# A 4096-cubed matmul with GELU on one core: more of its Strassen products split a second time

## The chip, the core and the metric

The kernel runs on one core of one Trainium2 chip. The metric is device time in microseconds, median of several executions. Single executions of one kernel agree within some 0.3%. A ratio is the mean time of one kernel's fast runs over that of the other's in the same rounds, so it is not quite the ratio of the medians quoted.

## The reference

```python
def reference(a, b):                      # float32, 4096 x 4096 each
    x = np.matmul(a, b)
    return 0.5 * x * (1 + np.tanh(np.sqrt(2 / np.pi) * (x + 0.044715 * x**3)))
```

## The kernel before

A and B are cut in quadrants and multiplied by Strassen's seven products (M1 to M7) in float16. The output is made in 16 groups, each a 512-row by 512-column tile of all four output quadrants. One product of one group is 64 matmuls of 128x128x512. It accumulates in one of two chains of four PSUM banks (the accumulators of TensorE), X or Y. A group goes in steps: a quarter of an unsplit product, or one of the half-sized products explained next.

From group 6 on, the right-hand operands come back from DRAM, where earlier groups kept them ("k_M", units of 1 MB), into a ring of eight 1 MB tiles ("bK"). A product can itself be split by Strassen into seven half-sized ones, 7/8 of the work. This is done for the pair M3/M5 in groups 11, 13, 14 and 15. For that, the first group that meets a set of columns after group 5 (the "maker": groups 6, 7, 9, 10) computes 14 right-hand halves of 0.5 MB. Ten of them are VectorE sums, made in one of three buffers "bS"; four are raw quarters. It writes all to DRAM ("k_split").

```python
SPLIT_GROUPS = (11, 13, 14, 15)
...
    def make_split(gi, s, p):
        blocks = [split_tiles[gi, nb, product(gi, s)[0], c] for c in range(CH)]
        o = SPLIT[p][2]
        if isinstance(o, str):
            t = quarter_b(blocks, o)
        else:
            t = pool.tile([P, 4 * NC], F16, name="bS", tag="bS", bufs=AHEAD + 1)   # 3 buffers
            take(t..., o[2], quarter_b(blocks, o[0]), quarter_b(blocks, o[1]))      # VectorE
        keep_operand((nb, "split", k // 2), k % 2, t)                               # SyncE queue
...
        makes = [                                     # one half of each product per step
            (position[gi, s + 1 + k // QPH, k % QPH], s, p)
            for s in (0, 1) for k, p in enumerate("1346725")
        ] if made else []
```

VectorE also makes the left-hand sums ("aS") that TensorE takes as weights, the joins of split products and the sums of the outputs, all in one order. The loads are issued by GpSimd, all writes by SyncE. Groups 9 and 10 also load A once more (float32, "stage"), to check the range of the inputs.

## Time and profile before

1574.95 us median of 3 runs (1574.2 to 1581.67). The profile shown has a span of 1580.3 us.

| | before |
|---|---|
| TensorE | 1561.8 us busy, 99% |
| VectorE | 1034.0 us, 65% |
| ScalarE | 656.7 us, 42% |
| DMA | 399.96 MB, 253 GB/s on average |

TensorE's busy time says that matmuls are running, not at what clock. The prediction shows the lines of each view. One more line shows groups 6 to 10 together; its columns are the stretch, its length, the busy time of TensorE, of weight loads, VectorE, ScalarE and GpSimd (with instructions), then the granted clock, the DMA share (the mean busy time of the 16 DMA engines over the stretch; it can come out above 1) and GB/s landed:

```profile
610.00:1102.00 492.00, 486.75 (x2242) 219.91 (x2241) 266.97 (x276) 208.54 (x650) 78.12 (x131) 0.99 0.99 284
```

### The profile page before, as it was taken

The numbers are of one execution on the slowest core, as the hardware profiler recorded it, in microseconds if no ns is written. First come the engines' busy times: TensorE is split into PE (matmuls) and PEld (weight loads), VectorE is DVE, ScalarE is ACT, GpSimd is POOL, SyncE is SP. The second block draws the span as 40 slices with busy tenths as digits, with TensorE's granted clock in tenths as the row PEclk, the third lists the DMA queues.
The fourth block names the chain that finished last, engine by engine and source line by source line (L and its number), as shares of the span: only waits on it lengthen the run. The fifth ranks groups of instructions, "written<-read, shape, count | busy, mean of one in ns | idle before, by whom it ended". The sixth has DMA issues, their size and how long they took to land. (4 is left out here: it accounts for less than half of the span.)

```text
span 1580.3 us, 21111 instructions
## 1 busy us (share of the span) xinstructions
PE 1561.8 (99%) x7630; PEld 748.3 (47%) x7630; DVE 1034.0 (65%) x1189; ACT 656.7 (42%) x1638; POOL 367.4 (23%) x652
## 2 busy tenths in 40 slices
PE   9999999999999999999999999999999999999998
PEld 4444444444444444444444444444644456474643
DVE  1697887969888886646454554476664574673853
ACT  1036444338874641212466435554456632121111
POOL 7763432331124300020222102201222101010100
PEclk9999999999999999999999999999999999999999
DMA  9999999994799986889999789999999667383752
GB/s 176 195 222 287 268 306 270 288 200 78 204 230 295 295 310 240 293 321 237 318 275 263 250 243 338 311 318 287 326 311 253 211 225 305 142 339 133 264 215 82
DMA packets 226336, 399.96 MB, mean 253 GB/s; under 512 B 17328, under 2 KB 156592, under 8 KB 204720
## 3 DMA queue, kind: packets, MB, share of 16 engines
q0 software_dynamic: 152704, 243.31, 65.1%
q1 hardware_dynamic: 73520, 155.22, 26.8%
q8 instruction: 62, 1.02, 0.2%
q14 instruction: 50, 0.41, 0.1%
HBM read 327.16 MB, written 155.19 MB: 305 GB/s over the span
## 5 line engine op out<-in xcount | busy, mean ns | idle before, releaser
L401 PEld LDWEIGHTS <-aS 128*128 128x128 f16 x4704 | 461.3, 98 | 565.9 <-issue 12.9
L401 PE MATMUL accX<-bK,aS 128*128 128x512 f16 x1664 | 360.9, 379 | 0.0
L763 DVE TENSOR_TENSOR aS<-aT 128x2048 f16<-128x2048 f16 x204 | 241.1, 1217 | 86.5 <-PE accX L401 57.8
L401 PE MATMUL accY<-bK,aS 128*128 128x512 f16 x1280 | 281.0, 382 | 5.2 <-DVE y L549 2.9
L401 PEld LDWEIGHTS <-aT 128*128 128x128 f16 x1728 | 169.3, 98 | 207.9 <-issue 4.8
L540 ACT ACTIVATE y<-y 128x512 f32<-128x512 f32 x192 | 119.0, 630 | 285.2 <-DVE y L549 285.1
L228 ACT ACTIVATE scrap<-stage 128x256 bf16<-128x256 f16 x512 | 212.8, 416 | 50.1 <-DMA stage<-in_a_dram 35.3
L206 POOL DMA_DIRECT2D bR<-in_b_dram x320 | 173.1, 544 | 208.0 <-DMA bR<-in_b_dram 112.5
L760 POOL DMA_DIRECT2D bK<-k_M x124 | 67.8, 548 | 515.7 <-PE accX L401 105.2
L206 POOL DMA_DIRECT2D stage<-in_a_dram x176 | 111.6, 642 | 231.0 <-ACT scrap L228 171.0
L365 DVE TENSOR_TENSOR aS<-aT 128x2048 f16<-128x2048 f16 (+1 forms) x112 | 133.9, 1200 | 34.6 <-PE accX L401 25.6
L401 PE MATMUL accX<-bS,aS 128*128 128x512 f16 x704 | 153.4, 379 | 1.3 <-ACT x L513 0.7
L513 ACT COPY x<-accX 128x512 f32<-128x512 f32 x128 | 74.6, 586 | 180.5 <-PE accX L401 174.4
L365 DVE TENSOR_TENSOR bS<-bR 128x2048 f16<-128x2048 f16 x110 | 133.6, 1217 | 16.6 <-PE accX L401 12.0
L250 ACT ACTIVATE square<-bR 128x1024 bf16<-128x1024 f16 x120 | 122.9, 1049 | 48.3 <-DVE energy L549 46.9
L401 PE MATMUL accX<-bK,aT 128*128 128x512 f16 x640 | 139.8, 379 | 0.0
L181 DVE STREAM_TRANSPOSE aT<-stage 128x2048 uint32<-128x2048 uint32 (+1 forms) x37 | 74.6, 2017 | 66.7 <-DMA stage<-in_a_dram 65.2
L513 ACT COPY m<-accX 128x512 f32<-128x512 f32 x60 | 34.5, 581 | 199.6 <-PE accX L401 179.3
L549 DVE TENSOR_TENSOR x<-x,x 128x512 f32<-128x512 f32 x64 | 43.7, 683 | 85.7 <-ACT x L513 85.7
L228 ACT ACTIVATION_READ_ACCUMULATOR scrap<-stage 128x1 f32 x512 | 95.5, 187 | 0.0
L549 DVE TENSOR_TENSOR energy<-energy,square 128x1024 bf16<-128x1024 bf16 x120 | 82.0, 683 | 9.7 <-ACT square L250 8.1
L549 DVE TENSOR_TENSOR x<-accX,x 128x512 f32<-128x512 f32 x64 | 43.6, 690 | 62.4 <-ACT y L540 56.0
(63 smaller groups left out, 1167.6 us busy)
## 6 DMA issues: line engine op xcount, KB each, us to landing
bK<-k_M POOLq DMA_DIRECT2D x124, 1024.0 KB, 10.5
out_dram<-y SPq DMA_DIRECT2D x256, 256.0 KB, 6.8
bR<-in_b_dram POOLq DMA_DIRECT2D x320, 128.0 KB, 7.5
k_M<-bS SPq DMA_DIRECT2D x80, 512.0 KB, 6.6
stage<-in_a_dram POOLq DMA_DIRECT2D x144, 256.0 KB, 10.6
bK<-k_split POOLq DMA_DIRECT2D x28, 1024.0 KB, 6.7
k_split<-bS SPq DMA_DIRECT2D x40, 512.0 KB, 4.8
k_M<-bR SPq DMA_DIRECT2D x16, 1024.0 KB, 12.1
```

The source lines that it names most:

```text
L181: nc.vector.transpose(dst[:, :, x, :], src[:, :, x, :])
L206: nc.gpsimd.dma_start(out=dst, in_=src)
L228: nc.scalar.activation(weighed[mb, quad, c][:, :RUN], s[:, x, :], ACT.Square, accum_out=weighed[mb, ih][:, k, x : x + 1])
L250: nc.scalar.activation(t[:, :], src, ACT.Square)
L365: nc.vector.tensor_tensor(out=x, in0=y, in1=z, op=ALU.add if o[2] > 0 else ALU.subtract)
L401: nc.tensor.matmul(acc[:, :], sa[:, j // 2, i * P : (i + 1) * P, j % 2], sb[:, j, :], start=start and j == 0, stop=stop and j == 3, skip_g ...
L513: nc.scalar.copy(out=t[:, :], in_=src[:, :])
L540: nc.scalar.activation(y[:, :], src[:, :], ACT.Gelu_apprx_tanh)
L549: nc.vector.tensor_tensor(out=o[:, :], in0=x[:, :], in1=y[:, :], op=op)
L760: nc.gpsimd.dma_start(out=t, in_=kept_unit(*key[1:])[:, :])
L763: nc.vector.tensor_tensor(out=t, in0=y, in1=z, op=ALU.add if op > 0 else ALU.subtract)
```

## The change

The intent is to give TensorE fewer matmul columns. M3/M5 are split in groups 8 and 12 too, and a second pair, M2/M1, in groups 6, 9, 10, 13 and 14. For these five groups the products stand in another order, in which M2 and M1 begin both PSUM chains anew. Each maker now makes 28 halves. A group that is both maker and user of M2/M1 makes them in its steps 1 to 5, reads them back a few steps later, and makes those of M3/M5 at its end, for which it loads M3 and M5 again.

```diff
+FRESH = [PRODUCTS[k] for k in (0, 1, 2)] + [
+    ("M2", "Y", ("21", "22", -1), "11"), PRODUCTS[3], ("M4", "Y", "22", ("21", "11", 1)),
+    ("M6", "X", ("21", "11", -1), ("11", "12", 1)),
+]
+MAKES = (1, 1, 1, 2, 2, 2, 3, 3, 3, 3, 4, 4, 5, 5)
-SPLIT_GROUPS = (11, 13, 14, 15)
+SPLITS = {M3_M5: (8, 11, 12, 13, 14, 15), M2_M1: (6, 9, 10, 13, 14)}
+LOAD_AHEAD = 10
...
-        if p in "24":
-            joins[chain, p] = pool.tile([P, NC], F32, name="join", tag="x1", bufs=RT)
+        if p == "2":
+            joins[chain] = pool.tile([P, NC], F32, name="join", tag="m5", bufs=2)
...
-        makes = [ (position[gi, s + 1 + k // QPH, k % QPH], s, p) for s in (0, 1) ... ]
+            if gi in SPLITS[M2_M1]:
+                orders = [(M2_M1, 3, 4, MAKES), (M3_M5, 0, 1, [step_number(gi, 5, 0) + x // 2 for x in range(14)])]
+            else:
+                orders = [
+                    (M3_M5, 0, 1, [step_number(gi, 2, 0) + x // 2 for x in range(14)]),
+                    (M2_M1, 5, 3, [step_number(gi, 6, 0) + x // 3 - 1 for x in range(14)]),
+                ]
... (settling of the new order, the planning of the ring, bank parity: left out)
```

More of the change, by code (lines that the diff above doesn't have):

```diff
@@ L56 @@
 PAIR = [(s, p) for ps in ("213", "45", "76") for s in (0, 1) for p in ps]
+MAKES = (1, 1, 1, 2, 2, 2, 3, 3, 3, 3, 4, 4, 5, 5)
+M3_M5, M2_M1 = 0, 3
 SPLIT_AHEAD = 6
 FETCH_AHEAD = 12
-SPLIT_GROUPS = (11, 13, 14, 15)
+SPLITS = {M3_M5: (8, 11, 12, 13, 14, 15), M2_M1: (6, 9, 10, 13, 14)}
+LOAD_AHEAD = 10
 CHECK_GROUP = 9
@@ L321, in product @@
     def product(gi, s):
-        return (LAST if gi == len(groups) - 1 else PRODUCTS)[s]
+        if gi == len(groups) - 1:
+            return LAST[s]
+        return (FRESH if gi in SPLITS[M2_M1] else PRODUCTS)[s]
     kept = {}
@@ L388, in half_path @@
     post = {}
+    x_banks = [0]
+    for gi in range(len(groups) - 1):
+        x_banks.append(x_banks[gi] if gi in SPLITS[M2_M1] else 1 - x_banks[gi])
     def bank(gi, chain, i):
-        par = (gi + (chain == "Y")) % 2
+        par = (x_banks[gi] + (chain == "Y")) % 2
         t = psum_pool.tile([P, NC], F32, name=f"acc{chain}", tag=f"bank{par}{i}")
@@ L454, in multiply @@
         name, chain = product(gi, s)[:2]
-        first = q == 0 and name in ("M3", "M5")
+        first = q == 0 and name in (("M3", "M5", "M2", "M1") if gi in SPLITS[M2_M1] else ("M3", "M5"))
         sa, sb = sums.pop((gi, s, q))
@@ L490, in multiply_split @@
                 settle(gi, name, i)
-        if p in "24":
-            joins[chain, p] = pool.tile([P, NC], F32, name="join", tag="x1", bufs=RT)
+        if p == "2":
+            joins[chain] = pool.tile([P, NC], F32, name="join", tag="m5", bufs=2)
         for r in range(RT // 2):
-            def join(p):
-                return joins[chain, p][:, r * NC // 2 : (r + 1) * NC // 2]
+            join = joins[chain][:, r * NC // 2 : (r + 1) * NC // 2]
             def joined(out, x, y, op):
@@ L500, in multiply_split @@
             if p == "2":
-                nc.scalar.copy(out=join("2"), in_=region(chain, "21", r))
+                nc.scalar.copy(out=join, in_=region(chain, "21", r))
             elif p == "3":
-                joined(join("2"), region(chain, "12", r), join("2"), ALU.subtract)
-                joined(join("2"), region(chain, "11", r), join("2"), ALU.add)
+                joined(join, region(chain, "12", r), join, ALU.subtract)
+                joined(join, region(chain, "11", r), join, ALU.add)
             elif p == "4":
-                nc.scalar.copy(out=region(chain, "22", r), in_=join("2"))
-                joined(join("4"), region(chain, "21", r), join("2"), ALU.add)
+                nc.scalar.copy(out=region(chain, "22", r), in_=join)
+                joined(join, region(chain, "21", r), join, ALU.add)
             elif p == "5":
-                joined(region(chain, "11", r), join("4"), region(chain, "12", r), ALU.subtract)
+                joined(region(chain, "11", r), join, region(chain, "12", r), ALU.subtract)
     def keep(tag, src, bufs):
@@ L554, in settle @@
         end = gi == len(groups) - 1
-        if name == "M5":
+        if gi in SPLITS[M2_M1] and name not in ("M5", "M7"):
+            settle_fresh(gi, name, i, X, Y)
+        elif name == "M5":
             if end:
@@ L587, in settle, with settle_fresh @@
             waiting.append((gi, i, 1, 1, y, y))
+    def settle_fresh(gi, name, i, X, Y):
+        if name == "M3":
+            post["x1", i] = keep("x1", Y, RT)
+        elif name == "M2":
+            m2, x1, x7 = keep("m5", Y, 2), post["x1", i], post["x7", i]
+            tt(x1, x1, m2, ALU.subtract)
+            tt(x7, x7, m2, ALU.subtract)
+        elif name == "M1":
+            m1, x7 = keep("m5", X, 2), post["x7", i]
+            tt(x7, x7, m1, ALU.add)
+        elif name == "M4":
+            emit(gi, i, 1, 0, new_y(), Y)
+            y = new_y()
+            tt(y, Y, post.pop(("x7", i)), ALU.add)
+            flush()
+            waiting.append((gi, i, 0, 0, y, y))
+        elif name == "M6":
+            y = new_y()
+            tt(y, X, post.pop(("x1", i)), ALU.add)
+            flush()
+            waiting.append((gi, i, 1, 1, y, y))
     steps = [(0, -1, n) for n in range(N_PLAIN)]
@@ L592, in half_path @@
     for gi in range(1, len(groups)):
-        if gi in SPLIT_GROUPS:
-            steps += [(gi, s, p) for s, p in PAIR]
-        else:
-            steps += [(gi, s, q) for s in (0, 1) for q in range(QPH)]
-        steps += [(gi, s, q) for s in range(2, NP) for q in range(QPH)]
+        s = 0
+        while s < NP:
+            if gi in SPLITS.get(s, ()):
+                steps += [(gi, s + x, p) for x, p in PAIR]
+                s += 2
+            else:
+                steps += [(gi, s, q) for q in range(QPH)]
+                s += 1
     position = {step: n for n, step in enumerate(steps)}
@@ L603, in step_number @@
         gi, s = gi + s // NP, s % NP
-        return position.get((gi, s, q), first_step[gi] + s * len(SPLIT) + 2 * q)
+        if (gi, s, q) in position:
+            return position[gi, s, q]
+        s0 = max(x for x in SPLITS if x <= s)
+        return position[gi, s0, PAIR[0][1]] + (s - s0) * len(SPLIT) + 2 * q
     def at(gi, s, q, fn, *args):
@@ L674, in do @@
             before.setdefault(n, []).append((fn, args))
+        free_at = [0, 0]
         for (quad, c), n in zip(chunks, turns):
-            do(n - 6, load, (load_a, (mb, quad, c)))
+            do(max(n - LOAD_AHEAD, free_at.pop(0)), load, (load_a, (mb, quad, c)))
+            free_at.append(n + 4)
             if turned:
@@ L736, in half_path @@
     )}
-    n_ring = 0
     tasks = {}
@@ L742, in task, with ring_place @@
         tasks.setdefault(n, []).append((fn, args))
-    def ring_place(need, ahead):
-        nonlocal n_ring
-        x = n_ring % len(ring)
-        n_ring += 1
-        n = max(ring_end[x] + 1, need - ahead)
+    owner = {}
+    def ring_place(need, ahead, key, after=0):
+        x = min(ring_end, key=ring_end.get)
+        n = max(ring_end[x] + 1, need - ahead, after)
         assert n <= need, (steps[need], steps[n])
+        owner[x] = key
+        ring_end[x] = need
         return x, n
@@ L771, in quarter_b, with blocks_a @@
         return tiles[k].rearrange("p (x y) -> p x y", x=NJ)[:, :, w * NC // 2 : (w + 1) * NC // 2]
-    def blocks_a(gi, o):
+    def blocks_a(gi, s, o):
         if isinstance(o, str):
@@ L777, in blocks_a, with open_block, block_sum @@
         return [
-            split_tiles["d", gi, c].rearrange("p (jj m) -> p jj m", jj=NJ // 2) for c in range(CH)
+            split_tiles["d", gi, s, c].rearrange("p (jj m) -> p jj m", jj=NJ // 2) for c in range(CH)
         ]
-    def open_block(gi, c, x):
-        split_tiles["d", gi, c] = ring_tile(x, "aD")
-    def block_sum(gi, o, q):
+    def open_block(gi, s, c, x):
+        split_tiles["d", gi, s, c] = ring_tile(x, "aD")
+    def block_sum(gi, s, o, q):
         w = 4 * NC
-        t = split_tiles["d", gi, q // 2][:, (q % 2) * w : (q % 2 + 1) * w]
+        t = split_tiles["d", gi, s, q // 2][:, (q % 2) * w : (q % 2 + 1) * w]
         mb = groups[gi][0]
@@ L795, in operand_a @@
             y, z, op = SPLIT[q][1]
-            blocks = blocks_a(gi, o)
+            blocks = blocks_a(gi, s, o)
             t = t.rearrange("p (jj m) -> p jj m", jj=NJ // 2)
@@ L811, in operands @@
             if sa is None:
-                sa = quarter_a(blocks_a(gi, oa), SPLIT[q][1])
-            k = PAIR.index((s, q))
-            sb = split_tiles[gi, nb, "split", k // 2][:, (k % 2) * w : (k % 2 + 1) * w]
+                sa = quarter_a(blocks_a(gi, s, oa), SPLIT[q][1])
+            k = PAIR.index((s - max(x for x in SPLITS if x <= s), q)) % 2
+            sb = split_tiles[split_key(gi, s, q)][:, k * w : (k + 1) * w]
         else:
@@ L823, in make_split @@
         nb = groups[gi][1]
-        blocks = [split_tiles[gi, nb, product(gi, s)[0], c] for c in range(CH)]
+        name = product(gi, s)[0]
+        blocks = [split_tiles[gi, nb, name, c] for c in range(CH)]
         o = SPLIT[p][2]
@@ L834, in make_split @@
             t = t[:, :]
-        k = PAIR.index((s, p))
-        keep_operand((nb, "split", k // 2), k % 2, t)
+        s0, x = {"M3": (M3_M5, 0), "M5": (M3_M5, 1), "M2": (M2_M1, 0), "M1": (M2_M1, 1)}[name]
+        k = PAIR.index((x, p))
+        keep_operand((nb, "split", s0, k // 2), k % 2, t)
     b_slot0 = dict(b_slot)
@@ L843, in half_path, with split_key, plan_fetch @@
     last_a = 0
+    made_at = {}
+    def split_key(gi, s, p):
+        s0 = max(x for x in SPLITS if x <= s)
+        return gi, groups[gi][1], "split", s0, PAIR.index((s - s0, p)) // 2
+    def plan_fetch(units, key, n, ahead):
+        if key not in units or owner[units[key]] != key:
+            units[key], e = ring_place(n, ahead, key, made_at.get(key[1:], -1) + 1)
+            task(e, fetch, key, units[key])
+        ring_end[units[key]] = max(ring_end[units[key]], n)
     for gi in range(N_RAW, len(groups)):
-        n0, nb = first_step[gi], groups[gi][1]
-        split = (gi, 0, "1") in position
+        nb = groups[gi][1]
         made = gi == maker[nb]
-        mine = [n for n in range(n0, first_step.get(gi + 1, len(steps)))]
+        mine = [n for n in range(first_step[gi], first_step.get(gi + 1, len(steps)))]
         ready = position[gi - 1, NP - 1, 2] if groups[gi][0] != groups[gi - 1][0] else 0
-        units, block_users = {}, []
-        makes = [
-            (position[gi, s + 1 + k // QPH, k % QPH], s, p)
-            for s in (0, 1) for k, p in enumerate("1346725")
-        ] if made else []
+        units, places, users = {}, {}, {}
+        makes = {}
+        if made:
+            if gi in SPLITS[M2_M1]:
+                orders = [(M2_M1, 3, 4, MAKES), (M3_M5, 0, 1, [step_number(gi, 5, 0) + x // 2 for x in range(14)])]
+            else:
+                orders = [
+                    (M3_M5, 0, 1, [step_number(gi, 2, 0) + x // 2 for x in range(14)]),
+                    (M2_M1, 5, 3, [step_number(gi, 6, 0) + x // 3 - 1 for x in range(14)]),
+                ]
+            for s0, y, x, whens in orders:
+                for k, ((z, p), n) in enumerate(zip(PAIR, whens)):
+                    if whens is MAKES:
+                        n += first_step[gi]
+                    makes.setdefault(n, []).append(((y, x)[z], p))
+                    made_at[nb, "split", s0, k // 2] = n
         for n in mine:
@@ L857, in half_path @@
             name, _, oa, ob = product(gi, s)
+            for sm, p in makes.get(n, ()):
+                for c in range(CH):
+                    key = (gi, nb, product(gi, sm)[0], c)
+                    plan_fetch(units, key, n, FETCH_AHEAD)
+                task(n, make_split, gi, sm, p)
+                if not isinstance(SPLIT[p][2], str):
+                    assert free["bS"][-AHEAD - 1] < n, steps[n]
+                    free["bS"].append(n)
             block = q in SPLIT and not isinstance(oa, str)
             if block and q == PAIR[0][1]:
-                places = [ring_place(n, SPLIT_AHEAD) for c in range(CH)]
-                e = max(ready, last_a, *(e for _, e in places))
-                for c, (x, _) in enumerate(places):
-                    task(e, open_block, gi, c, x)
+                places[s] = [ring_place(n, SPLIT_AHEAD, (gi, s, c)) for c in range(CH)]
+                users[s] = []
+                e = max(ready, last_a, *(e for _, e in places[s]))
+                for c, (x, _) in enumerate(places[s]):
+                    task(e, open_block, gi, s, c, x)
                 for qq in range(QPH):
-                    task(e, block_sum, gi, oa, qq)
+                    task(e, block_sum, gi, s, oa, qq)
                 last_a = e
@@ L870, in half_path @@
             if not isinstance(o, str):
-                tag = "aS" if made or n_a % 2 else "bS"
+                ahead = SPLIT_AHEAD if q in SPLIT else AHEAD
+                only = any(n - ahead <= x <= n for x in makes) or made and q not in SPLIT
+                tag = "aS" if only or n_a % 2 else "bS"
                 n_a += 1
-                e = max(n - (SPLIT_AHEAD if q in SPLIT else AHEAD), ready, last_a, free[tag][-AHEAD - 1] + 1)
+                e = max(n - ahead, ready, last_a, free[tag][-AHEAD - 1] + 1)
                 assert e <= n, steps[n]
@@ L878, in half_path @@
             if block:
-                block_users.append(max(e, n if isinstance(o, str) else 0))
-                for x, _ in places:
-                    ring_end[x] = max(block_users)
+                users[s].append(max(e, n if isinstance(o, str) else 0))
+                for x, _ in places[s]:
+                    ring_end[x] = max(users[s])
             task(n, operands, gi, s, q)
-            key = (gi, nb, "split", PAIR.index((s, q)) // 2) if q in SPLIT else (gi, nb, name, q // 2)
-            if key not in units:
-                units[key], e = ring_place(n, FETCH_AHEAD)
-                task(e, fetch, key, units[key])
-            ring_end[units[key]] = max(n, *(e for e, s1, _ in makes if s1 == s)) if s < 2 and made else n
-        for e, s, p in makes:
-            task(e, make_split, gi, s, p)
-            if not isinstance(SPLIT[p][2], str):
-                free["bS"].append(e)
+            key = split_key(gi, s, q) if q in SPLIT else (gi, nb, name, q // 2)
+            plan_fetch(units, key, n, FETCH_AHEAD)
     with tc.manual_schedule():
```

## The prediction

> **What bounds the kernel now.** I read the page's first two parts first: which engine is busy, and how evenly.
>
> ```profile
> PE 1561.8 (99%) x7630; PEld 748.3 (47%) x7630; DVE 1034.0 (65%) x1189; ACT 656.7 (42%) x1638; POOL 367.4 (23%) x652
> DMA  9999999994799986889999789999999667383752
> ```
>
> TensorE is busy 99% of the span with almost no holes, so today the number of matmul columns sets the time. But the second line says that the DMA engines are nearly as full in slices 11 to 31. The list of what TensorE waited for confirms the first: all its waits come to some 13 us, and the chain of waits is useless here (one Gelu).
>
> ```profile
> PE accY L401 <- DVE y L549: 5.1, 3, 2.9
> PE accY L401 <- DVE bS L365: 2.4, 1, 2.4
> PE accY L401 <- DMA bK<-k_M: 2.3, 1, 2.3
> ```
>
> What a split is worth is in the timeline of TensorE at group 11, which splits M3 and M5 already (start, length, instruction):
>
> ```profile
> 1101.91 3.87 PE L483 MATMUL accY<-bK,aS 128*128 128x512 f16 x32
> 1105.61 1.91 PE L483 MATMUL accY<-bK,aT 128*128 128x256 f16 x16
> 1107.36 3.87 PE L483 MATMUL accX<-bK,aS 128*128 128x512 f16 x32
> ...
> 1126.79 27.79 PE L401 MATMUL accX<-bK,aS 128*128 128x512 f16 x128
> 1154.41 13.98 PE L401 MATMUL accX<-bK,aT 128*128 128x512 f16 x64
> ```
>
> The split pair runs from 1101.91 to 1126.79, 24.88 us; the next two products unsplit from 1126.79 to 1154.41, 27.62 us. So a split pair saves 2.74 us, and the second step (1105.61 to 1107.36 for 16 narrow matmuls) gives 109 ns each against 216 ns for a wide one.
>
> Last, the DMA, by stretches. The first two lines below are groups 6 and 7, then 8, 9, 10 (boundaries from the TensorE timeline); 1292 to 1386 is group 13.
>
> ```profile
> 610.00:707.00 97.00, 97.00 (x451) 43.95 (x450) 51.00 (x55) 16.80 (x29) 6.97 (x13) 1.00 0.76 283
> 707.00:809.00 102.00, 99.07 (x446) 44.24 (x445) 58.77 (x58) 42.85 (x136) 20.66 (x34) 0.97 1.03 279
> 809.00:906.00 97.00, 97.00 (x451) 43.98 (x450) 48.99 (x51) 53.73 (x177) 18.10 (x30) 1.00 1.09 259
> 906.00:1005.00 99.00, 96.69 (x449) 43.73 (x448) 50.71 (x55) 43.39 (x136) 18.14 (x30) 1.00 1.03 293
> 1005.00:1102.00 97.00, 97.00 (x451) 44.02 (x450) 57.49 (x61) 51.77 (x175) 14.25 (x24) 1.00 1.02 307
> 1292.00:1386.00 94.00, 94.00 (x546) 53.25 (x544) 56.41 (x71) 19.43 (x37) 9.14 (x17) 1.00 0.63 235
> 972.00:984.00 12.00, 9.69 (x46) 4.31 (x44) 5.12 (x6) 10.01 (x35) 5.33 (x9) 1.00 1.01 420
> 20.00:90.00 70.00, 69.70 (x323) 31.40 (x322) 40.06 (x44) 7.16 (x13) 52.99 (x94) 1.00 1.34 196
> ```
>
> The last two numbers are the DMA share and GB/s landed. The two bottom lines give the plateaus: 420 GB/s when kept f16 operands and outputs move, and only 196 GB/s when float32 inputs are loaded and cast (each landed byte is two read, so 392 read). Groups 7 to 10 already sit at a share of 1.02 to 1.09.
>
> **What the Trainium skill says.** "TensorE: Matmul & The Clock Gate", Back-to-back issue gap: N/2.4 + 2.5 ns warm, so 215.8 and 109.2 ns for 512 and 256 columns; the trace agrees (216 and 109), so halving the columns costs only 1.3 ns a matmul. Same page, Part 1: an array idle for some 3.4 us falls to half clock. The trace has it: after the 2.93 us wait at 792.59 the next 64 matmuls took 16.76 us instead of 13.82. "DMA: Bandwidth & Descriptors", Specifications: fabric ceiling 435 GB/s and an HBM limit of about 358 per core. The plateau of 420 agrees with the first and not with the second; I use 420. Same page, Measured: 1 MB takes 6.15 us alone; here the median landing of a 1 MB kept unit is 6.7 us (split units) and 10.5 us (others, in fuller stretches).
>
> **The change part by part.**
>
> TensorE. Two more M3/M5 pairs are split (groups 8 and 12) and five M2/M1 pairs (6, 9, 10, 13, 14): 7 x 2.74 = 19.2 us less. This is certain and lies wholly on the path.
>
> VectorE. From the two built programs: 110 more sums of 128x2048 at 1.217 us (row L763) = 134 us, and 112 more joins at 0.42 us (row L498) = 47 us; the settling operations keep their number. 1034 + 181 = 1215 us, 78% of 1556. In groups 6, 9 and 10 it is about 31 us more on some 51 to 57, about 85 of 94 us: full, though not over.
>
> ScalarE: 40 more copies at 0.58 and 56 at 0.37, together 44 us, to 45%. Harmless. PSUM: the fresh start of M2 and M1 takes the banks that M3/M5 and M7 left one product earlier (13.8 us), for four copies of 0.58 us: enough. The join tiles now share the tag of the M5 copies, used long before.
>
> DMA. From the built programs: 45 more loads of 1.05 MB (49 split units more, 4 others fewer) = 47 MB, and 56 more writes of split halves at 0.52 MB = 29 MB; 400 MB become 476 MB. Most of it falls in groups 6 to 10, which make the kept splits: each of the four makers (6, 7, 9, 10) writes 28 halves instead of 14, and 6, 9 and 10 read M3 and M5 a second time and read back within the group what they have just written. Placing loads and writes by the step at which they are planned:
>
> Groups 6 to 10 before: 69 loads (72 MB), 56 half writes (29 MB), outputs 21 MB, staging 16 chunks (17 MB). (72 + 29 + 21)/0.42 = 291 us, plus 17/0.2 = 84 us: 375 us of work in the 491 us that these groups take. It fits.
>
> After: 103 loads (108 MB), 112 halves (59 MB), outputs 21, staging 17: (108 + 59 + 21)/0.42 = 447, plus 84: 531 us, in the 473 us that TensorE would want (5 x 96.7 less 4 x 2.74). It does not fit.
>
> By group, work against TensorE's time: 6: 102 against 94; 7: 98 against 97; 8: 83 against 94; 9: 133 against 94 (25 loads, 28 half writes, and five chunks of staging, which here serve the check); 10: 113 against 94. The ring holds 8 MB and loads are planned 10 to 20 us ahead, so a group can't borrow from one far away. The overruns alone sum to 8 + 1 + 39 + 19 = 67 us. Groups 11 to 15 stay under (about 78 of 94 at most), so there the gain arrives.
>
> I take the floor of the added stall as 58 us (all idle time used) and the ceiling as about 110 (before, the engines were occupied for about 430 us, from two-microsecond stretches, for what I count as 375, so the rate is not always the plateau). My choice is 72 us, near the sum of overruns, since some writes are not urgent. The loads of staging now go up to 10 steps ahead instead of 6; that may take away part of the 5.9 us lost in group 7 (2.93 of wait and 2.94 of slow clock), and I allow 3 us.
>
> Sum: 1575 - 19 - 3 + 72 = 1625 us.
>
> **The rivals.**
>
> First, TensorE stays the bound and the DMA fits after all: 1575 - 19 - up to 8 of old stalls = 1548 to 1556, within 2%. For it: TensorE is at 99%, and a tuned kernel would hardly be given work that doesn't fit. Against it: 531 us of transfers at the best rate seen; to fit, the rate would have to be some 12% above the plateau, or much of the writing deferred past group 10, which the three bS buffers do not allow.
>
> Second, VectorE becomes the bound in 6, 9 and 10: ten sums for the kept M2/M1 splits come in five steps (17 us), need 12 us, and use three buffers, each free only after its write (4.8 us median, longer under load). In order behind them stand the left-hand sums of M5. This would cost perhaps 5 us in each of the three groups, 1570 if it came alone. It adds little to a DMA bound, as it is the same waiting.
>
> Third, only short lead: within the M2/M1 pairs units are planned just 10.5 us ahead (15.6 at least before). If a 1 MB unit takes 10.5 us or more under load, each of the five pairs stalls for a few microseconds even where the average fits: 10 to 20 us, total about 1570. I think that it is true for 6, 9 and 10 and not for 13 and 14, whose DMA share is 0.63 now.
>
> **Range and chances.** The low end, 1575, is a stall that only cancels the gain; the high end, 1685, is the ceiling of stalls plus slow-clock time after them. Faster by 2% (under 1543) would need more than the split and all old stalls together give: 0.01. Slower by 2% is over 1606, a net stall of 53 us, just under my floor: 0.75. Within: 0.24.
>
> **What would show it.** Right: TensorE's busy share falls to about 95%, with waits on bK units from DMA (and sums held by them) in groups 6, 9 and 10, the most in 9; the DMA share there over 1.0 with some 400 GB/s where float32 isn't loaded; groups 6 to 10 last about 70 us longer than 473; and every split pair in 12, 13 and 14 at 24.9 us with no wait. Total landed about 476 MB. Wrong: groups 9 and 10 at 94 us each with TensorE full. That would mean that the plateau isn't a ceiling, or that I have placed transfers in the wrong groups.

## The result, and the profile after

The changed kernel takes 1720.24 us (1717.14 to 1720.92, 4 runs) against 1577.4 us, ratio 1.09, 95% interval 1.0866 to 1.0933: slower by 9%. It was outside the predicted range, on the side that the prediction favoured. The page of the changed kernel, busy times and the DMA by slices:

```profile
PE 1579.7 (92%) x8302; PEld 822.2 (48%) x8302; DVE 1197.6 (70%) x1411; ACT 696.2 (41%) x1734; POOL 391.4 (23%) x697
DMA  9999999937999798999998989999999987676862
```

TensorE's share fell from 99% to 92%: 139.1 us of the span without a matmul instead of 18.5. Its busy time did not fall by the 19.2 us of saved columns, it rose by 17.9; I put the 37 us between down to matmuls at a lower clock after waits (the granted clock in groups 6 to 10 is 0.92 instead of 0.99). VectorE, ScalarE and DMA come close to what was counted in the built programs (1215 us, 701 us and 476 MB; measured 1197.6, 696.2 and 476.6).

The stretches of the changed kernel: first groups 6 to 10 in one line, then each of them, then group 11. Same columns as above:

```profile
611.00:1239.00 628.00, 509.03 (x2626) 264.03 (x2624) 373.62 (x415) 231.52 (x706) 97.43 (x168) 0.92 1.02 326
...
611.00:729.00 118.00, 100.16 (x547) 53.92 (x545) 79.23 (x91) 23.92 (x45) 13.48 (x25) 0.94 0.91 340
729.00:850.00 121.00, 99.08 (x447) 43.91 (x445) 70.33 (x66) 41.81 (x134) 19.55 (x33) 0.94 1.13 331
850.00:955.00 105.00, 99.59 (x546) 55.67 (x547) 66.25 (x80) 57.23 (x187) 20.17 (x34) 0.95 1.01 293
955.00:1095.00 140.00, 105.65 (x546) 55.59 (x544) 76.28 (x87) 56.80 (x182) 25.52 (x43) 0.88 1.05 316
1095.00:1239.00 144.00, 104.55 (x545) 54.95 (x544) 81.53 (x94) 51.77 (x160) 18.70 (x34) 0.88 0.98 342
1239.00:1339.00 100.00, 97.44 (x545) 54.81 (x544) 72.06 (x81) 45.92 (x144) 22.27 (x37) 0.97 1.05 286
```

Groups 6 to 10 take 628 us instead of 492, and 326 GB/s over them are 205 MB instead of 140: the 65 MB that were counted. That is 136 of the 138.5 us by which the profiled spans differ. Group 11 loses 6 us and 12 one, while 13 and 14 gain 2.7 each. The DMA share is about 1 throughout, but the rate is 293 to 342 GB/s, well under the plateau of 420.

What TensorE waited for, by total, number and longest:

```profile
PE accX L417 <- DVE aS L811: 57.9, 14, 7.6
PE accY L417 <- DMA bK<-k_M: 16.2, 7, 10.5
PE accY L499 <- DVE aS L811: 13.1, 2, 8.8
PE accY L417 <- DVE aS L811: 12.5, 2, 11.1
PE accX L417 <- DMA bK<-k_M: 10.0, 1, 10.0
```

The largest part is left-hand sums of VectorE (aS), 85 us with one small group not shown, and only some 30 us are loads. VectorE is at 70%, so it isn't too slow; it stands still. Its own waits in the whole program:

```profile
DVE bS L811 <- DMA k_split<-bS: 133.7, 32, 16.4
```

In the kernel before there is no such line: the row of these sums in its view of groups ends with 0.0 us of idle time (after the count come busy us and mean ns):

```profile
L763 DVE TENSOR_TENSOR bS<-bK 128x2048 f16<-128x2048 f16 x40 | 48.3, 1217 | 0.0
```

How the two meet is in the timelines at the start of group 10, first TensorE, then VectorE (start, length, instruction, and in brackets the idle time before it and what ended that):

```profile
1112.33 9.13 PE L417 MATMUL accY<-bK,aT 128*128 128x512 f16 x32 [10.51 <-DMA bK<-k_M]
1129.07 5.85 PE L417 MATMUL accX<-bK,aS 128*128 128x512 f16 x16 [7.61 <-DVE aS L811]
1141.26 27.29 PE L417 MATMUL accX<-bK,aS 128*128 128x512 f16 x112 [6.35 <-DVE aS L811]
```

```profile
1106.79 3.48 DVE L811 TENSOR_TENSOR bS<-bK 128x2048 f16<-128x2048 f16 x3
1126.65 1.23 DVE L811 TENSOR_TENSOR bS<-bK 128x2048 f16<-128x2048 f16 x1 [16.37 <-DMA k_split<-bS]
1127.79 1.22 DVE L811 TENSOR_TENSOR aS<-aT 128x2048 f16<-128x2048 f16 x1
1128.93 1.22 DVE L811 TENSOR_TENSOR bS<-bK 128x2048 f16<-128x2048 f16 x1
1138.85 1.22 DVE L811 TENSOR_TENSOR bS<-bK 128x2048 f16<-128x2048 f16 x1 [8.70 <-DMA k_split<-bS]
1139.99 1.22 DVE L811 TENSOR_TENSOR aS<-aT 128x2048 f16<-128x2048 f16 x1
```

VectorE fills its three buffers by 1110, then stands 16.37 us until a write has emptied one. The left-hand sum that TensorE needs is the next instruction in its order. It needs no write and no load; it runs at 1127.79, and TensorE goes on at 1129.07. The same happens again 12 us later. The loads are held by it too: a block of the ring can be overwritten only when the sums that read it are done, and GpSimd stood 117.1 us (9 times) before loads for these sums of VectorE, against 32.5 us in the kernel before. The 10.51 us above end with such a load: GpSimd waited 14.14 us and issued it at 1104.78, just after the sum at 1103.26, for which VectorE had stood 9.34 us. The Trainium skill says in "TensorE: Matmul & The Clock Gate", Part 1 (the array as 16 sub-arrays, queue depths), that ScalarE and VectorE take their instructions strictly first in, first out; the trace agrees, as the ready sum did not pass the blocked one. The first line of TensorE also shows the slow clock: 32 matmuls took 9.13 us, where after a short wait they take 7.07.

What the splits save arrived where the DMA has room. Group 13, M3/M5:

```profile
1436.79 3.87 PE L499 MATMUL accY<-bK,aS 128*128 128x512 f16 x32
...
1461.67 13.98 PE L417 MATMUL accX<-bK,aS 128*128 128x512 f16 x64
1475.48 3.87 PE L499 MATMUL accY<-bK,aS 128*128 128x512 f16 x32
```

1461.67 - 1436.79 is 24.88 us, as before, with no wait.

### The profile page after: what moved, and what is told of

The parts are those of the page before. It is cut to its first block, busy times and chain, and to the rows that moved or that the text cites. A ratio compares the mean times of both kernels' runs of the same rounds, so it can differ in the third digit from the quotient of the medians.

```text
span 1718.8 us, 23125 instructions
## 1 busy us (share of the span) xinstructions
PE 1579.7 (92%) x8302; PEld 822.2 (48%) x8302; DVE 1197.6 (70%) x1411; ACT 696.2 (41%) x1734; POOL 391.4 (23%) x697
## 5 line engine op out<-in xcount | busy, mean ns | idle before, releaser
L417 PEld LDWEIGHTS <-aS 128*128 128x128 f16 x3936 | 388.9, 99 | 570.1 <-DVE aS L811 78.5
L417 PEld LDWEIGHTS <-aT 128*128 128x128 f16 x1600 | 157.6, 99 | 211.2 <-issue 23.3
L555 ACT ACTIVATE y<-y 128x512 f32<-128x512 f32 x192 | 118.9, 629 | 325.1 <-DVE y L564 315.5
L811 DVE TENSOR_TENSOR aS<-aT 128x2048 f16<-128x2048 f16 x166 | 196.7, 1217 | 24.1 <-PE accX L417 20.5
L499 PEld LDWEIGHTS <-aS 128*128 128x128 f16 x1760 | 176.6, 101 | 62.4 <-DVE aS L811 16.3
L811 DVE TENSOR_TENSOR bS<-bK 128x2048 f16<-128x2048 f16 x80 | 96.4, 1220 | 144.0 <-DMA k_split<-bS 133.7
L417 PE MATMUL accY<-bK,aS 128*128 128x512 f16 x640 | 141.4, 383 | 13.4 <-DVE aS L811 12.5
L417 PE MATMUL accY<-bK,aT 128*128 128x512 f16 x576 | 129.9, 387 | 15.2 <-DMA bK<-k_M 15.2
L808 POOL DMA_DIRECT2D bK<-k_split x77 | 41.7, 543 | 446.8 <-PE accX L417 125.9
L499 PE MATMUL accY<-bK,aS 128*128 128x256 f16 (+1 forms) x880 | 108.8, 283 | 20.1 <-DVE aS L811 13.1
L528 ACT COPY x<-accX 128x512 f32<-128x512 f32 x108 | 62.9, 586 | 138.1 <-PE accX L417 132.0
L499 PE MATMUL accX<-bK,aS 128*128 128x256 f16 (+1 forms) x880 | 108.8, 283 | 8.7 <-DMA bK<-k_split 4.2
```

The lines of the kernel that those rows point to most:

```text
L417: nc.tensor.matmul(acc[:, :], sa[:, j // 2, i * P : (i + 1) * P, j % 2], sb[:, j, :], start=start and j == 0, stop=stop and j == 3, skip_g ...
L499: nc.tensor.matmul(banks[chain, i][:, :] if wide else out, sa[:, j // 2, r * P : (r + 1) * P, j % 2], sb[:, : NC] if wide else sb[:, j * N ...
L528: nc.scalar.copy(out=t[:, :], in_=src[:, :])
L555: nc.scalar.activation(y[:, :], src[:, :], ACT.Gelu_apprx_tanh)
L808: nc.gpsimd.dma_start(out=t, in_=kept_unit(*key[1:])[:, :])
L811: nc.vector.tensor_tensor(out=t, in0=y, in1=z, op=ALU.add if op > 0 else ALU.subtract)
```

## The experiments

Two theories stood. Theory 1: the transfers of groups 6 to 10 do not fit. Theory 2: what costs is the order, with VectorE in line behind three buffers, whatever the bytes. Seventeen kernels ran; all gave correct results. Edits are against the changed kernel unless said otherwise. Kernels ran beside the kernel before, whose median was 1575.6 to 1576.6.

**e1_m3m5: the M3/M5 part alone.**

```diff
-SPLITS = {M3_M5: (8, 11, 12, 13, 14, 15), M2_M1: (6, 9, 10, 13, 14)}
+SPLITS = {M3_M5: (8, 11, 12, 13, 14, 15), M2_M1: ()}     # and no halves of M2/M1 are made
```

> Only the M3/M5 part of the change (groups 8, 11 to 15); no M2/M1 splits and none of their kept halves. Theory 1, too many bytes for the DMA engines in groups 6 to 10: these bytes are nearly those of before, so the two added pairs give 2 x 2.74 us and the time is about 1570 us (1564 to 1577), no long waits of TensorE. Theory 2, order: two halves are now made per step instead of one, and VectorE stands in line behind the three bS buffers whatever the bytes; then some 5 us are lost in each of the four makers and the time is about 1585 to 1595.

1592.14 us, ratio 1.0100 (1.0083 to 1.0117). Two pairs more than before and still 16 us slower, as theory 2 expected. Of what the change adds in bytes, only some loads in 8 and 12 are left. VectorE waited 58.3 us for writes of bS, and TensorE up to 6.8 us for an aS sum. So something other than bytes costs; e7_pace shows that it is the order.

**e2_late: M2/M1 in groups 13 and 14 only.**

```diff
+SPLITS = {M3_M5: (8, 11, 12, 13, 14, 15), M2_M1: (13, 14)}   # halves made where used: groups 7 and 9
```

> All M3/M5 splits, and M2/M1 split in groups 13 and 14 only, kept halves of M2/M1 made only where used (groups 7 and 9). Theory 1: four added pairs give 11 us; group 7 just fits and group 9 is over by about 12 us (staging for the check): about 1575 to 1580. Theory 2: these makers make M2/M1 late (three halves in three steps at M6), so the start of a group isn't held up; about 5 us in each of two makers: about 1575. Both expect groups 13 and 14 without waits.

1634.31 us, ratio 1.0365. Both theories missed by 55 us. From the end of group 7 on, where three halves are made per step beside float32 staging, TensorE waited 3.6, 9.3 and 7.3 us for aS; from the end of group 9 on, 6.6, 8.4 and 7.1 us. VectorE waited 114.8 us for bS writes. So a late burst costs too, not only an early one.

**e3_check: the check's staging moved from 9 and 10 to 13 and 14.**

```diff
-CHECK_GROUP = 9
+CHECK_GROUP = 13
```

> The changed kernel with the staging for the check moved from groups 9 and 10 to 13 and 14. Bytes are the same, their place isn't. Theory 1: 7 MB of float32 staging at 200 GB/s leave groups 9 and 10, so about 35 us of stalls go there, and 13 and 14 have room: about 1685 us. Theory 2: the kept halves are made as before, so at most 10 us: about 1710.

1709.02 us, ratio 1.0841. 11 us less than the changed kernel, where theory 1 expected 35. With these bytes gone from 9 and 10, VectorE still waited 118.9 us for its buffers, and small new waits came in 13 and 14.

**e4_dram: raw quarters copied from DRAM to DRAM.**

```diff
+        if isinstance(o, str):                     # source: the kept operand, not the fetched block
+            t = kept_unit(nb, name, h)...[:, :, w * NC // 2 : (w + 1) * NC // 2]
```

> The changed kernel, with the raw quarters of the kept splits copied from the kept operand in DRAM instead of from the fetched block in SBUF. Bytes as before, but the SyncE queue no longer waits for fetched blocks to land (102 us of its waits) in front of the other writes and the outputs. Theory 1: same bytes, 1710 to 1720. Theory 2: the writes from bS go out as soon as VectorE has made them, VectorE waits clearly less than 134 us for them, and the time falls by 20 us or more, to 1700 or less.

1717.58 us, ratio 1.0895. Under 3 us less. VectorE's wait went from 133.7 to 123.6 us only. The SyncE queue's waits for fetched blocks were not what held the writes back.

**e5_m2m1: M3/M5 only in groups 8 and 13.** The makers 6, 9 and 10 then write 14 halves instead of 28.

```diff
+SPLITS = {M3_M5: (8, 13), M2_M1: (6, 9, 10, 13, 14)}     # halves made only where used
```

> M2/M1 split in the five groups of the change, M3/M5 only in 8 and 13, so that the makers 6, 9 and 10 write 14 halves instead of 28 and do not read M3 and M5 again. Theory 1 (bytes): group 6 then has 75 us of transfers for 94 us, group 10 has 85, only group 9 is over, by 12 us: 1575 - 8 (three more pairs than before) + 12, about 1580 us. Theory 2 (order: VectorE in line behind three bS buffers): the first five steps of 6, 9 and 10 are as in the changed kernel, whose waits there were 6, 11 and 14 us, and the slow clock after them comes on top: 1610 us or more.

1666.13 us, ratio 1.0558. The first steps of 6 and 9 have much the same waits as in the changed kernel (0.5 to 3.1 us in 6, up to 8.2 us in 9), now with fewer bytes, which favours theory 2; in 10 they are shorter (1.2 to 4.8 us instead of 6.4 to 10.5). But the whole is 54 us faster than the changed kernel, though it saves 11 us less of columns. So what was left out at the groups' ends costs as well; it is bytes and sums in VectorE's order at once, and this run does not part them.

**e6_join: own join tiles.** Against e1_m3m5; M3/M5's second join tile of the kernel before is restored.

> The M3/M5 part alone (1592 us), with the second join tile of the kernel before given back to M3/M5, so that VectorE's joins do not wait for ScalarE's copy out of the same tile. Its trace had two waits of 4.35 and 3.78 us for such a join in groups 8 and 12, and slow clock after them. If the shared tile is the cause: 1592 - 8 to 12, about 1582. If the cause is that VectorE or ScalarE is late anyway (staging in those groups), 1590.

1596.67 us, ratio 1.0139. The two waits stayed at 4.35 and 3.77 us: the shared tile is not their cause.

**e7_pace: one half per step.** Against e6_join.

```diff
-                    (M3_M5, 0, 1, [step_number(gi, 2, 0) + x // 2 for x in range(14)]),
+                    (M3_M5, 0, 1, [step_number(gi, 2, 0) + x for x in range(14)]),
```

> As the run with the second join tile, and the kept halves of M3/M5 made one per step instead of two. The same bytes. Theory 2: VectorE waits much less than 58 us for its bS buffers, the 6.8 us wait at M2 of group 9 goes with its slow clock, and the time is some 9 us less than in the run with the join tile alone, about 1573. Theory 1: no change beyond 2 us.

1582.44 us, ratio 1.0044 (1.0026 to 1.0062). 14 us less at the same bytes, and VectorE's wait for writes of the kept halves fell from 59.3 us to 4.3. What is left are the two waits of the joins. In group 8 of this kernel, the timelines of VectorE and then of TensorE:

```profile
812.79 0.26 DVE L246 TENSOR_REDUCE stat_a<-rows 128x16 f32<-128x64 f32 x1 [5.15 <-ACT scrap L238]
812.97 1.66 DVE L521 TENSOR_TENSOR join<-accY,join 128x256 f32<-128x256 f32 x4
...
821.33 2.30 DVE L191 STREAM_TRANSPOSE aT<-stage 128x2048 uint32<-128x2048 uint32 x1
823.56 1.18 DVE L819 TENSOR_TENSOR aS<-aD 128x2048 f16<-128x2048 f16 x1
824.66 0.75 DVE L521 TENSOR_TENSOR accY<-join,accY 128x256 f32<-128x256 f32 x2
```

```profile
825.14 6.53 PE L499 MATMUL accY<-bK,aS 128*128 128x256 f16 x32 [3.94 <-DVE accY L521]
```

The same pattern: VectorE stands 5.15 us for a reduction of row sums that ScalarE has not finished. The joins behind it run late, and TensorE waits 3.94 us for the last of them.

**e8_room: seven buffers.** Against e3_check; in groups 6, 9 and 10 the two idle staging buffers of 8 KB per partition serve as four more buffers for kept halves.

```diff
-            t = pool.tile([P, 4 * NC], F16, name="bS", tag="bS", bufs=AHEAD + 1)
+            t = make_room(gi)     # 3 of 7 sums to bS, 4 to halves of the two "stage" buffers
```

> The changed kernel with the check's staging in 13 and 14 (1709 us), and the two staging buffers, which are then unused in groups 6, 9 and 10, lent to the kept halves, so that VectorE has seven buffers to write to instead of three. Same bytes, same pace. Theory 2: VectorE's wait for buffers (119 us) falls by more than half, group 6 falls from 118 us to 106 or less, the whole to 1670 or less. Theory 1: the writes still take their time, and TensorE waits for loads instead: 1695 to 1710.

1687.69 us, ratio 1.0717. 21 us less than e3_check at the same bytes and pace. VectorE's wait for bS fell from 118.9 to 34.8 us, and the waits in the first steps of 6 and 9 are gone. But group 6 still takes 110 us (expected 106 or less), and the whole did not reach 1670. The waits are now at the ends: 12.4, 12.5 and 15.3 us in M6 of 6, 9 and 10. VectorE there waits for output tiles instead (61.0 us for writes of the output). More buffers take away most of the waits of order at the groups' starts; what is left at the ends was not parted further.

**e9_weigh: the reduction later.** Against e7_pace.

```diff
-                do(n + 4, weigh_half, mb, int(quad[0]) - 1)
+                do(min(n + 9, turns[4]) if quad == "12" else n + 4, weigh_half, mb, int(quad[0]) - 1)
```

> The M3/M5 part with its own join tiles and one half per step (1582 us), and the reduction of the check's row sums, for which VectorE stood 5.15 us in groups 8 and 12 in front of the joins, put up to five steps later. If that place in VectorE's order is what makes TensorE wait 3.9 and 3.8 us for a join there, both waits go with the slow clock after them: about 1572 us, just under before. If not, 1582.

1575.98 us, ratio 0.9994 (0.9977 to 1.0011). The waits of 3.94 and 3.78 us became 1.52 and 1.47. The place in VectorE's order was most of the cause, and moving one small instruction was worth some 8 us (ratio 1.0044 to 0.9994). The gain of 5.5 us over before did not appear; waits of 0.4 to 2.3 us from group 8 on, 9 us in sum in the profiled run, stand against it.

**e10_both and e11_best: both causes removed, with a mistake.**

> M2/M1 split in five groups, M3/M5 only in 8 and 13 (1666 us), with both causes taken away from groups 6, 9 and 10 at once: few bytes there (no kept M3/M5 halves, the check in 13 and 14) and seven buffers for VectorE's sums. If these two are all of it, 6, 9 and 10 take 94 to 98 us each, only group 7 (28 halves, staging, three buffers) stays some 25 us too long, and the time is about 1595 us. If the fresh order itself (both chains begun anew, the m5 copies) costs anything, these groups stay over 100 us and the time over 1615.

> As the run with both causes removed, and group 7's kept halves of M2/M1 made in group 8 instead, spread over twelve steps, M3/M5's at one per step, own join tiles, the reduction later. Seven split pairs for the four of before, 8.2 us: if everything else is hidden, about 1568 us, which would beat before; if group 8 is now too full (14 writes beside 21 loads and staging), 1580.

1669.67 and 1662.79 us. These do not test what they were meant to. My edit let group 9 use the second half of a staging buffer opened in group 6, so that buffer stayed occupied and groups 7 and 8 had one staging buffer: VectorE waited 80 and 85 us for staging.

**e15_traffic: the bytes alone.** Against the kernel before; one dead copy of 0.5 MB from DRAM to DRAM at each of the 140 steps of groups 6 to 10.

```diff
+            if 6 <= step[0] <= 10:
+                x = n % 14
+                nc.sync.dma_start(
+                    out=idle[x][:, :], in_=kept_unit(x % 4, "M7", 0)[:, : 4 * NC]
+                )
```

> The kernel before, plus one copy of half a MB from DRAM to DRAM at each of the 140 steps of groups 6 to 10: 73 MB, about what the change adds there (65 MB), with no engine's work depending on it. If the bytes alone make the stalls: 72 + 29 + 21 + 73 MB at 420 GB/s and 17 MB at 200 GB/s are 548 us for 491 us, so at least 57 us more, 1632 us or more, with TensorE waiting for loads. If bytes can be absorbed and the order of waiting made the loss: under 1600.

1703.02 us, ratio 1.0797 (1.0774 to 1.0819). Nothing is computed differently, and it costs 126 us. Groups 6 to 10, then TensorE's longest waits by sum:

```profile
610.00:1218.00 608.00, 511.37 (x2235) 224.22 (x2234) 259.64 (x270) 206.59 (x648) 78.05 (x131) 0.91 1.08 345
```

```profile
PE accY L401 <- DMA bK<-k_M: 39.6, 4, 10.3
PE accX L401 <- DVE aS L763: 16.7, 5, 7.7
PE accX L401 <- ACT m L513: 13.6, 1, 13.6
```

The stretch takes 608 us instead of 492, at 345 GB/s, 210 MB. Here loads are the largest part of TensorE's waits, 47 of some 108 us, against 30 of some 134 in the changed kernel. Bytes that no computation needs cost most of what the change lost, and about twice my floor of 57 us. Two things keep this from being the bytes of the change and nothing else. A copy inside DRAM both reads and writes it, 147 MB of DRAM traffic more, where the change adds 77. And the copies stand in SyncE's line before the outputs; they waited there 68 us for earlier copies.

**e13_both: e10_both without the mistake** (the count of buffers starts anew in each group).

> M2/M1 in five groups, M3/M5 in 8 and 13, check in 13, seven buffers in 6, 9 and 10; the earlier run of this without the mistake that kept a staging buffer occupied. If few bytes and enough buffers are all that the makers need: 6, 9 and 10 at 94 to 98 us, group 7 alone some 25 us too long, about 1595 us in all. If the fresh order costs something itself: over 1615.

1625.82 us, ratio 1.0313. Groups 9 and 10 in the view of stretches:

```profile
938.00:1033.00 95.00, 94.98 (x549) 53.56 (x548) 68.00 (x81) 24.45 (x46) 11.27 (x21) 1.00 0.96 355
1033.00:1127.00 94.00, 94.00 (x546) 53.28 (x545) 67.67 (x80) 23.84 (x45) 13.91 (x25) 1.00 0.99 354
```

They take TensorE's own time, 94 us, with no wait, where the changed kernel had 140 and 144. So the fresh order costs nothing itself, and few bytes with enough buffers are all that these two needed. Group 6 took 100 us. Groups 7 and 8, which had three buffers and a late burst, took 229 us together, where TensorE's own time is 191. The total missed 1595 for that and for three waits of 2.6 to 4.7 us in group 13, to which the check was moved.

**e14_best: e11_best without the mistake.**

> The same, with group 7 relieved (M2/M1's halves of its columns made in group 8 over twelve steps, M3/M5's one per step), own join tiles, the reduction later; without the mistake. Seven split pairs for four, 8.2 us: about 1568 us if all is hidden, so just better than before; 1580 if group 8 is too full.

1601.72 us, ratio 1.0146. Relieving group 7, with own join tiles and the later reduction, gained 24 us more, but waits of 2 to 5 us in groups 7 to 9 and 13 remain. It beats neither its expectation nor the kernel before.

**e12_one: e9_weigh with M2/M1 in group 13**, its halves made in group 8 over twelve steps.

> The M3/M5 part with the later reduction, and M2/M1 split in group 13 alone, its halves made in group 8 over twelve steps. Theory: a fresh-order group without a maker's burst costs nothing, so 2.7 us less than the same without it, about 1569; if the 7 MB more written in group 8 beside its staging hold VectorE or the loads, 1575 to 1580.

1578.31 us, ratio 1.0016 (1.0001 to 1.0032). No gain. The next run suggests that 14 writes beside a split and staging are too much for group 8.

**e16_pick: e12_one without the split of M3/M5 in group 8.**

> The M3/M5 splits in 11 to 15 (one pair more than before), M2/M1 in group 13 with its halves made in group 8, which now has no split of its own; one half per step, own join tiles, the reduction later. Two pairs more than before, 5.5 us, and no maker with a burst: if the transfers of group 8 are hidden, 1569 to 1572 us, a little better than before; if not, as before, 1576.

1569.51 us (1567.31 to 1576.19, 6 runs), ratio 0.9964 (0.9936 to 0.9993). This beats both kernels, the one before by 0.4%. It splits six pairs instead of four and has no burst in any maker.

**e17_later: the dead copies in groups 12 to 15.** As e15_traffic, 130 copies.

> The kernel before plus 130 dead copies of half a MB (68 MB) in groups 12 to 15 instead of 140 in 6 to 10. There the transfers at the plateau rates come to 204 us, 366 with the copies, for 379 us of TensorE; with the 11% over the plateau count that the run with copies in 6 to 10 showed, 406. If the place decides: 0 to 30 us more than before (1577 to 1607). If dead copies cost the same anywhere: over 1670.

1607.50 us, ratio 1.0193. 68 MB cost 31 us here and 73 MB cost 126 us in 6 to 10. So the place decides: group 13, for one, had a DMA share of 0.63 before.

## Why the prediction was right or wrong

The direction, the place and the counts were right. Slower was the favoured outcome; the bytes landed were 476 MB; groups 6 to 10 carry the loss; the pairs of 13 and 14 ran at 24.9 us (that of 12 took 28.8, with a wait of 3.78 us for a join); the saving of 2.74 us a pair was exact. The wait was the most in 10 (50 us over TensorE's own time), not in 9 (46). Of its other signs, TensorE's share is 92% and not 95%, the rate in group 6, which stages almost no float32, is 340 GB/s and not some 400, and most waits are for sums, not for loads.

**The step that failed** is "I take the floor of the added stall as 58 us (all idle time used) and the ceiling as about 110", and "My choice is 72 us". The loss to be explained is 143 + 19 = 162 us, of which 628 - 472.5 = 155 us lie in groups 6 to 10. Two terms were mis-sized.

First, the bytes. I took the room left in groups 6 to 10 as 492 less a computed 375, 117 us. But the two-microsecond stretches, each counted with its DMA share but at most 1, had shown the engines occupied for about 430 us of it. The room was 62 us. 65 MB at the plateau are 155 us; 430 + 155 = 585 us, 113 more than TensorE's 472. Counted in the same way, the engines were occupied for 581 us in the changed kernel, and for 600 us with the dead copies, where 430 us and 70 MB give 597, in spite of their double DRAM traffic. The run of dead copies also fits the size in time: 70 MB more landed in that stretch and 116 us more were taken, so 65 MB are some 108 us. I had this number in hand as my "ceiling" and chose the floor's side of it. Plateaus of 420 and 196 GB/s held in short stretches; over 608 saturated us the mixture moved 345.

Second, the rival "VectorE becomes the bound", of which I wrote "It adds little to a DMA bound, as it is the same waiting." It is not the same waiting. By this account some 42 to 47 us of the 155 are left for order (155 less 108 to 113). That split is a subtraction, not a measurement; it fits that the DMA engines had nothing to do for 47 of the 628 us (628 less 581). What runs do show of order at equal bytes is 21 us (e3_check to e8_room) and 14 us (e6_join to e7_pace). Where every load is in time, a write with no urgency still stops TensorE, since VectorE holds a ready sum behind it. I gave it 5 us in each of three groups.

The third rival, short leads, was right as far as it went: the M2/M1 pairs of groups 13 and 14 had no waits with leads of 10.5 us. In 6, 9 and 10, where it was expected, there is one such wait, of 4.19 us in 9. "ScalarE: Harmless" was wrong in groups 8 and 12, where its late row sums held VectorE and so the joins (e9_weigh). ScalarE did not get slower: VectorE stood 5.47 us for these sums in groups 8 and 12 of the kernel before too, but there no split stood behind it. The join tiles were harmless, as said (e6_join). The allowance of 3 us for earlier staging can't be seen: group 7 took 121.7 us instead of 102.7. What stays open is how much of the slow clock, 37 us of busy time, is on the path: while transfers are the bound, a slower TensorE costs nothing.

## What to carry to other kernels

TensorE at 99% says what bounds the kernel now, not what room the rest has. Read the room as the DMA's observed idle time in the very groups that get the new bytes; a computed minimum of its work overstates it. Here one split pair saves 2.74 us of TensorE, and 14 kept halves alone need 7.3 MB, 17 us of DMA at 420 GB/s. And a producer that shares an in-order engine with the critical path needs buffers for the latency of its slowest consumer under load, or a slow pace, or it stops work that is ready.

## What the Trainium skill lacked or had wrong

- "DMA: Bandwidth & Descriptors", Where 436 GB/s comes from, says that for transfers between HBM (the chip's DRAM) and SBUF the HBM limit of about 358 GB/s per core binds. This core landed 420 GB/s over 12 us. The page's Measured section fits: 425 GB/s with the pair's other core idle, and about 358 when both stream. So the prediction set its 420 against a figure that is for two busy cores.
- The same page has no rate that I found for loads that cast float32 to float16: 196 GB/s landed over 70 us, at a DMA share of 1.34. Nor did I find what a saturated mixture sustains: 345 GB/s over 608 us in the run of dead copies.
- "TensorE: Matmul & The Clock Gate", Part 1, gives some 3.4 us of idle time to half clock. Waits of 2.93 us (before) and 3.09 us (changed kernel, 16 matmuls in 5.02 us instead of 3.63) were already followed by slow matmuls, and one of 3.73 us was not (32 in 7.08 us). A free-running window, which the page describes, would allow the last, since a wait of that length can straddle two windows. It does not explain the first two, in which no whole window fits; so the prediction's "The trace has it", said of 2.93 us, was too quick.
